# The first two weight tiles in column halves over two DMA queues, and the first output tile in one transfer

## The chip, the cores and the metric

The kernel runs on one core of one Trainium2 chip. The core has a matrix engine (TensorE, PE in the profile), whose weight loads have a row of their own (PEld), a vector engine (VectorE, DVE), a scalar engine (ScalarE, ACT), GpSimd (POOL) and a sync engine (SyncE, SP) that here only starts transfers. DMA transfers are started by SP's and by ScalarE's instruction stream; each stream works in order, so a transfer that has to wait before it may start holds back everything behind it on that stream, on ScalarE its activations too. The metric is the device time of one execution in microseconds (us).

## The reference

The reference is a decoder trunk of two layers on 256 tokens of width 1024, all in float32. Layer 0 is a feed-forward block, a gated linear recurrence, and a second feed-forward block; layer 1 is a feed-forward block, attention with a forget gate, and a second feed-forward block. Each sub-layer is normed before and after. Cut to what the change touches, the first block of layer 0 and the last sum:

```python
def rms_norm(x, g):
    y = x * lax.rsqrt(jnp.mean(x * x, axis=-1, keepdims=True) + EPS)
    return y * g

def swiglu(x, w_gate, w_up, w_down):
    return (jax.nn.silu(x @ w_gate) * (x @ w_up)) @ w_down

f = swiglu(rms_norm(h, ffn1_pre_g[layer]), ffn1_w_gate[layer], ffn1_w_up[layer], ffn1_w_down[layer])
h = h + 0.5 * rms_norm(f, ffn1_post_g[layer])
...
f = swiglu(rms_norm(h, ffn2_pre_g[layer]), ffn2_w_gate[layer], ffn2_w_up[layer], ffn2_w_down[layer])
h = h + 0.5 * rms_norm(f, ffn2_post_g[layer])
return h
```

`w_gate` and `w_up` are 1024 x 2816, `w_down` is 2816 x 1024.

## The kernel before

The 256 tokens are two row tiles, t = 0 and t = 1, of 128 tokens each. A float32 product is made of three products of rounded parts: each weight tile is loaded as `raw` and split into `whi` (a rounded copy, on ScalarE, or on VectorE where `dve=True`) and `wlo` (what the copy lost, on VectorE), and the inputs likewise into `xhi` and `xlo`; TensorE then adds whi x xhi, wlo x xhi and whi x xlo into one bank. A weight unit `i` is a `raw` tile of 128 x 1024, which for the gate weights holds two row blocks of 128 x 512 (index `a` = 0 and 1). Five `raw` buffers take turns.

Nearly all of the kernel is planned by a small cost model (`prepare_next`, `slot`, `run`), which decides when a unit is loaded and split. TensorE's order is the program's. The opening, lines 1097 to 1214, is written out by hand, in this manner:

- `load_h(t, a, b)` (line 108) loads columns of row blocks a to b of the input rows of tile t into `h[t]`; `load_w(i, a, b)` (line 1101) loads row blocks a to b of weight unit i. Lines 1106 to 1116 start them, on SP unless ScalarE's queue is named.
- `turn` (1132) transposes blocks of `h` on TensorE, `x_up` (1138) and `x_lo` (1143) make `xhi` and `xlo` of them with the gains `gT`; `w_up` (1119) and `w_lo` (1126) split the weights.
- `products(t, i, order)` (1149) issues the matmuls. In "0ul" the digit is the row block of the unit, the first letter says `whi` (u) or `wlo` (l), and the second `xhi` (u) or `xlo` (l).
- `keep_busy(n)` (121) issues n matmuls of 128 x 512 on constants, whose result nothing reads. There are six at the start and three after the first two transposes.

TensorE's stream there is: six idle matmuls, the gains' transpose, two transposes of `h[0]`, three idle matmuls, five products of (t 0, unit 0), the transposes `turn(1, 0, 2)` and `turn(1, 2, 4)` of the rows of tile 1, the sixth product, `turn(0, 2, 4)`, the six products of (1, 0), and the products of (0, 1), the first two of which read row block 0 of unit 1 and the third row block 1. ScalarE's stream is: start the load of the gains, a first activation that loads its table, start row block 1 of unit 0, start blocks 0 to 4 of `h[1]`, start row block 1 of unit 1, then the first `x_up`.

[...] In the built program the first transfers stand so (SP's and ScalarE's own order from top to bottom):

| queue | transfer | counter | must wait for |
|---|---|---|---|
| ScalarE | gains | 0 | - |
| ScalarE | unit 0, block 1 | 5 | - |
| ScalarE | h[1], blocks 0 to 4 | 7 | - |
| ScalarE | unit 1, block 1 | 1 | h[0], blocks 0 to 2 |
| SP | h[0], blocks 0 to 2 | 1 | - |
| SP | unit 0, block 0 | 2 | - |
| SP | h[0], blocks 2 to 4 | 3 | - |
| SP | unit 1, block 0 | 4 | - |
| SP | h[0], blocks 4 to 8 | 6 | - |
| SP | unit 2 | 0 | gains |
| SP | h[1], blocks 4 to 8 | 2 | unit 0, block 0 |
| SP | unit 3 | 3 | h[0], blocks 2 to 4 |

At the end `enter(t, ..., last=True)` (line 257) takes the sums of squares of the last block's output (ScalarE), the norm's factor (VectorE and GpSimd), and adds the normed product to `h[t]` in pieces (line 281), each of which is stored when it is done (line 283). Tile 0 comes some microseconds ahead of tile 1.

Of the kernel before, what the change touches and what calls it, by code (L numbers as in the profile page):

```python
# [16 lines left out]
P = 128  # L17
# [27 lines left out]
def trunk_kernel(ctx: ExitStack, tc: tile.TileContext, A: dict, out: bass.AP):  # L45
    nc = tc.nc
# [11 lines left out]
    def nm(s):  # L58
        uid[0] += 1
        return f"{s}_{uid[0]}"  # L60
# [4 lines left out]
    def gtbank():  # L65
        return psum.tile([P, 512], F32, tag="gt", name=nm("gt"), bufs=2)

    def trbank():
        return psum.tile([P, 512], F32, tag="tr", name=nm("tr"), bufs=2)
# [11 lines left out]
    def defer(n, fn):  # L81
        pend.append([n, fn])
# [23 lines left out]
    h = [hpool.tile([P, D], F32, tag=f"h{t}", name=f"h{t}") for t in range(2)]  # L106

    def load_h(t, a, b, q=nc.sync):

        q.dma_start(h[t][:, a * P:b * P], A["x"][0, t * P:(t + 1) * P, a * P:b * P])  # L110
# [10 lines left out]
    def keep_busy(n):  # L121

        ps = trbank()
        for _ in range(n):
            nc.tensor.matmul(ps, nc.const_aps.tensor(1.0, (P, P), BF16), nc.const_aps.tensor(1.0, (P, 512), BF16),
                             start=True, stop=True)
# [24 lines left out]
    def new_raw():  # L151
        return wpool.tile([P, 1024], F32, tag="raw", name=nm("raw"), bufs=RAW)
# [40 lines left out]
    def rstd_of(ss, n, f=1.0, add=nc.gpsimd):  # L193

        v = spool.tile([P, 1], F32, tag="nv", name=nm("nv"))
        add.tensor_scalar(v, ss[:, 0:1], ss[:, 1:2] if n == 2 else 0.0, D * EPS * f * f, ALU.add, ALU.add)  # L196
        r = spool.tile([P, 1], F32, tag="rstd", name=nm("rstd"), bufs=8)
        nc.gpsimd.tensor_tensor(r, v, mhalf, ALU.pow)
        return r

    def square_sum(src, acc, f=1.0):
        junk = spool.tile([P, D], BF16, tag="junk", name=nm("junk"), bufs=1)
        nc.scalar.activation(junk[:, :src.shape[1]], src, AF.Square, scale=f, accum_out=acc)  # L203

    def new_ss():
        return spool.tile([P, 2], F32, tag="ss", name=nm("ss"))

    def to_tp(src, n):

        tp = gtbank()  # L210
        for j in range(4):
            nc.tensor.transpose(tp[:, j * P:(j + 1) * P], src[:, n * 512 + j * P:n * 512 + (j + 1) * P], ident)  # L212
        return tp
# [14 lines left out]
    def to_x(tps, dest):  # L228

        with tc.high_priority():  # L230
            xg = [x_upper(tps[n], dest, n) for n in range(2)]
            for n in range(2):
                x_lower(xg[n], dest, n)

    def to_x_tiles(tps, dest):

        gi, xh, xl = dest

        def operands(k):
            return tps[k // 4][:, k % 4 * P:(k % 4 + 1) * P], gT[:, gi + k:gi + k + 1]  # L240
        with tc.high_priority():
            for k in range(8):
                src, g = operands(k)
                nc.scalar.activation(xh[:, k, :], src, AF.Copy, scale=g)
            for k in range(8):
                src, g = operands(k)
                nc.vector.scalar_tensor_tensor(xl[:, k, :], src, g, xh[:, k, :].bitcast(F32), ALU.mult, ALU.subtract)  # L247
# [4 lines left out]
    def stat(t):  # L252
        ss = new_ss()
        square_sum(h[t], ss[:, 0:1])
        rs[t] = rstd_of(ss, 1)

    def enter(t, dests, pf, gb, half, last=False, normed=False):

        f = 1.0 / 16 if half else 1.0 / 32
        ss = new_ss()  # L260
        t1 = []
        urgent = tc.high_priority()
        urgent.__enter__()
        for n in range(2):
            square_sum(pf[n], ss[:, n:n + 1], f)
        for n in range(2):
            if n == 1 and last:
                r = rstd_of(ss, 2, f, nc.vector)
            t1.append(hpool.tile([P, 512], F32, tag="t1", name=nm("t1"), bufs=2))
            nc.vector.tensor_tensor(t1[n], pf[n], gb[:, n * 512:(n + 1) * 512], ALU.mult)  # L270
        if not last:
            r = rstd_of(ss, 2, f)

        sp, aq = nc.sync, nc.scalar
        pieces = [(n * 512, 512, None) for n in range(2)]
        if last:
            pieces = ([(0, 256, sp), (256, 256, sp), (512, 512, sp)] if t == 0 else
                      [(0, 256, sp), (256, 256, aq), (512, 256, sp), (768, 256, aq)])
        for c, m, q in pieces:
            hn, tn = h[t][:, c:c + m], t1[c // 512][:, c % 512:c % 512 + m]  # L280
            nc.vector.scalar_tensor_tensor(hn, tn, r[:, 0:1], hn, ALU.mult, ALU.add)
            if last:
                q.dma_start(out[0, t * P:(t + 1) * P, c:c + m], hn)
        urgent.__exit__(None, None, None)
        if last:
            return

        def inputs():
            tps = [to_tp(h[t], n) for n in range(2)]
            for dest in dests:  # L290
                to_x(tps, dest)
            stat(t)

        def norm():
            with tc.high_priority():
                normed_x()

        def normed_x():
            ss = new_ss()
            for n in range(2):  # L300
                square_sum(h[t][:, n * 512:(n + 1) * 512], ss[:, n:n + 1])
            rs[t] = rstd_of(ss, 2)
            hn = []
            for n in range(2):
                hn.append(hpool.tile([P, 512], F32, tag="t1", name=nm("hn"), bufs=2))
                nc.vector.tensor_scalar(hn[n], h[t][:, n * 512:(n + 1) * 512], rs[t][:, 0:1], None, ALU.mult)

            def go():
                tps = []
                for n in range(2):  # L310
                    tp = gtbank()
                    for j in range(4):
                        nc.tensor.transpose(tp[:, j * P:(j + 1) * P], hn[n][:, j * P:(j + 1) * P], ident)
                    tps.append(tp)
                to_x_tiles(tps, dests[0])
            defer(6, go)

        if normed:
            norm()
            settled[0] = True  # L320
        else:
            defer(3, inputs)
# [156 lines left out]
    def ffn_items(pool_of, wg, wu, wd, post_g, next_dests, last=False, normed=False):  # L479
# [52 lines left out]
        def post_down(t, accs):  # L532
            enter(t, next_dests(t), accs, box["gb"], True, last, normed)
# [47 lines left out]
    sp = rw.tile([RT, NRT], F32, name="sp")  # L581
# [279 lines left out]
    def get_yy(t, k):  # L861
# [3 lines left out]

    row_items(A["rg_w_out"][0], [width(i) for i in range(NRT)], get_yy,
              lambda t, accs: enter(t, [main_dest(GI[("ffn2", 0)], t)], accs, gbox["mix0"], False))
    ahead(n_rg, load_gb("mix0", A["mix_post_g"][0]))
    n_wout = len(items)
# [206 lines left out]
    for n in range(2):  # L1076
        proj_items(A["attn_w_q"][0], n * 512, 512, main_x, post_q(n))
    n_q[0] = len(items)
    row_items(A["attn_w_o"][0], [P] * 8, lambda t, k: (att["oh"][t][:, k, :], att["ol"][t][:, k, :]),
              lambda t, accs: enter(t, [main_dest(GI[("ffn2", 1)], t)], accs, gbox["mix1"], False), rows0=1, late=True)  # L1080
    ahead(n_q[0] + 2, load_gb("mix1", A["mix_post_g"][1]))
    n_att = len(items)
# [16 lines left out]
    raws = [new_raw() for _ in range(OPEN)]  # L1099

    def load_w(i, a, b, q=nc.sync):

        q.dma_start(raws[i][:, a * 512:b * 512].rearrange("p (k n) -> p k n", k=b - a),
                          A["ffn1_w_gate"][0, (2 * i + a) * P:(2 * i + b) * P, :512].rearrange("(k p) n -> p k n", p=P))

    load_h(0, 0, 2)
    load_w(0, 0, 1)
    load_w(0, 1, 2, nc.scalar)
    load_h(0, 2, 4)
    load_h(1, 0, 4, nc.scalar)  # L1110
    load_w(1, 0, 1)
    load_w(1, 1, 2, nc.scalar)
    load_h(0, 4, 8)
# [18 lines left out]
    def turn(t, a, b, bank):  # L1132

        for k in range(a, b):
            tps[t, k] = bank[:, (k - a) * P:(k - a + 1) * P]
            nc.tensor.transpose(tps[t, k], h[t][:, k * P:(k + 1) * P], ident)

    def x_up(t, a, b):
        for k in range(a, b):
            nc.scalar.activation(xhi[:, k, t * P:(t + 1) * P], tps[t, k], AF.Copy,  # L1140
                                 scale=gT[:, k:k + 1])
# [19 lines left out]
    gains_T(grow0, 16, 0)  # L1161
    turn(0, 0, 1, gtbank())
    turn(0, 1, 2, gtbank())
    keep_busy(3)
    x_up(0, 0, 2)
    w_up(0, 0, 1, dve=True)
    x_lo(0, 0, 1)
# [138 lines left out]
```

## Time and profile before

| | us |
|---|---|
| median of 3 runs | 998.65 (997.85 to 998.85) |
| the profiled execution's own time | 998.38 |
| its span | 996.7 |
| TensorE busy in the span | 987.9 (99%) |
| VectorE busy | 619.2 (62%) |
| ScalarE busy | 535.8 (54%) |
| GpSimd busy | 47.6 (5%) |

The span is what the profile records, and 1.7 us of the execution lie outside it. Matmuls are pipelined: a row's duration holds the time in which a matmul drains beside the next one, so that the spacing of the starts tells how fast TensorE works. A row of the timeline gives the start, the duration, the engine (a name with a q is that engine's instruction stream, which starts transfers), the line, the operation, its tiles, how many were merged, and in brackets how long the engine had been idle and what ended that. The rows of DMA queues give packets, megabytes and the share of 16 DMA engines' time in the stretch asked for; q1 is SP's queue and q10 ScalarE's (the bytes of each match the transfers that it starts).

### The profile page before, as it was taken

The numbers are of one execution on the slowest core, as the hardware profiler recorded it, in microseconds if no ns is written. First come the engines' busy times: TensorE is split into PE (matmuls) and PEld (weight loads), VectorE is DVE, ScalarE is ACT, GpSimd is POOL, SyncE is SP. The second block draws the span as 40 slices with busy tenths as digits, with TensorE's granted clock in tenths as the row PEclk, the third lists the DMA queues.
The fourth block names the chain that finished last, engine by engine and source line by source line (L and its number), as shares of the span: only waits on it lengthen the run. The fifth ranks groups of instructions, "written<-read, shape, count | busy, mean of one in ns | idle before, by whom it ended". The sixth has DMA issues, their size and how long they took to land.

```text
span 996.7 us, 12904 instructions
## 1 busy us (share of the span) xinstructions
PE 987.9 (99%) x4776; PEld 821.1 (82%) x4776; DVE 619.2 (62%) x792; ACT 535.8 (54%) x753; POOL 47.6 (5%) x92
## 2 busy tenths in 40 slices
PE   9999999999999999999999999999999999999997
PEld 6888888899988888888898888888888788888886
DVE  6756554668997555554686655554488875555542
ACT  7546443569986544443564444444366755444431
POOL 2400000100004000000100000000020010000000
PEclk9999999999999999999999999999999999999999
DMA  8867555565336766555457666555552366665531
GB/s 285 312 187 209 187 190 189 153 194 160 109 112 218 216 183 191 189 187 188 128 202 230 184 181 186 187 188 190 170 171 64 113 205 211 190 190 190 182 115 42
DMA packets 92645, 178.89 MB, mean 179 GB/s; under 512 B 11966, under 2 KB 32614, under 8 KB 92582
## 3 DMA queue, kind: packets, MB, share of 16 engines
q1 hardware_dynamic: 90998, 176.89, 56.3%
q10 hardware_dynamic: 752, 1.06, 0.3%
q8 instruction: 37, 0.61, 0.3%
q0 software_dynamic: 832, 0.12, 0.1%
q14 instruction: 26, 0.21, 0.1%
HBM read 176.95 MB, written 1.05 MB: 179 GB/s over the span
## 4 chain that ended last, share of the span: by engine, by line
PE 95%; DMA 1%; issue 1%; DVE 1%; POOL 0%; ACT 0%; POOLq 0%; DVEq 0%; ACTq 0%
PE mm L181 28%; PE mm L183 28%; PE mm L182 28%; PE tr L508 2%; PE gt L736 2%; PE gt L1027 1%; PE mm L188 1%; PE mm L190 1%; PE mm L189 1%; PE mm L1155 1%; PE mm L1062 1%; PE tr L1048 1%; DMA raw<-in_ffn_w_gate_dram 1%; PE gt L212 1%; DMA qT<-mone 0%
## 5 line engine op out<-in xcount | busy, mean ns | idle before, releaser
L175 DVE TENSOR_TENSOR wlo<-raw,whi 128x1024 fp32r<-128x1024 f32 (+4 forms) x329 | 395.3, 1207 | 270.0 <-ACT whi L171 267.3
L171 ACT ACTIVATE whi<-raw 128x1024 fp32r<-128x1024 f32 (+4 forms) x329 | 342.0, 1045 | 312.9 <-PE mm L183 250.9
L181 PE MATMUL mm<-whi,xhi 128*128 128x512 f32 (+2 forms) x768 | 304.0, 396 | 0.0
L183 PE MATMUL mm<-whi,xlo 128*128 128x512 f32 (+2 forms) x768 | 298.8, 389 | 0.0
L182 PE MATMUL mm<-wlo,xhi 128*128 128x512 f32 (+2 forms) x768 | 298.1, 388 | 0.0
L183 PEld LDWEIGHTS mm<-whi,xlo 128*128 128x128 f32 x768 | 144.2, 188 | 30.5 <-DVE xlo L247 0.3
L182 PEld LDWEIGHTS mm<-wlo,xhi 128*128 128x128 f32 x768 | 144.4, 188 | 28.0 <-DVE wlo L175 0.3
L181 PEld LDWEIGHTS mm<-whi,xhi 128*128 128x128 f32 x768 | 144.3, 188 | 27.5
L181 PE MATMUL mm<-whi,hhi 128*128 128x512 f32 x352 | 139.1, 395 | 0.0
L183 PE MATMUL mm<-whi,hlo 128*128 128x512 f32 x352 | 137.8, 391 | 0.0
L182 PE MATMUL mm<-wlo,hhi 128*128 128x512 f32 x352 | 136.9, 389 | 0.0
L183 PEld LDWEIGHTS mm<-whi,hlo 128*128 128x128 f32 x352 | 66.1, 188 | 14.9
L182 PEld LDWEIGHTS mm<-wlo,hhi 128*128 128x128 f32 x352 | 66.1, 188 | 14.1
L181 PEld LDWEIGHTS mm<-whi,hhi 128*128 128x128 f32 x352 | 66.2, 188 | 13.1
L502 DVE SCALAR_TENSOR_TENSOR prod<-mm,rstd,sil 128x512 f32<-128x512 f32 (+1 forms) x48 | 33.9, 705 | 38.0 <-PE mm L183 34.3
L493 ACT ACTIVATE sil<-mm,rstd 128x512 f32<-128x512 f32 (+1 forms) x48 | 31.2, 652 | 40.9 <-PE mm L183 40.5
L196 POOL TENSOR_SCALAR nv<-ss 128x1 f32<-128x1 f32 x22 | 10.7, 488 | 725.7 <-ACT junk L203 725.7
L512 ACT ACTIVATE hhi<-tr 128x512 fp32r<-128x512 f32 (+1 forms) x48 | 26.6, 554 | 15.6 <-PE tr L508 15.4
L270 DVE TENSOR_TENSOR t<-mm,gb 128x512 f32<-128x512 f32 x24 | 16.2, 685 | 24.9 <-ACT junk L203 24.7
L513 DVE TENSOR_TENSOR hlo<-tr,hhi 128x512 fp32r<-128x512 f32 (+1 forms) x48 | 30.5, 641 | 1.4
L203 ACT ACTIVATE junk<-mm 128x512 bf16<-128x512 f32 x24 | 14.3, 596 | 31.5 <-PE mm L183 31.4
L181 PE MATMUL mm<-whi,zhi 128*128 128x340 f32 (+2 forms) x80 | 28.3, 354 | 0.0
(193 smaller groups left out, 910.9 us busy)
## 6 DMA issues: line engine op xcount, KB each, us to landing
raw<-in_ffn_w_down_dram SPq DMA_DIRECT2D x88, 512.0 KB
raw<-in_ffn_w_up_dram SPq DMA_DIRECT2D x80, 512.0 KB
raw<-in_ffn_w_gate_dram SPq DMA_DIRECT2D x78, 512.0 KB
raw<-in_rg_w_in_dram SPq DMA_DIRECT2D x20, 504.0 KB
raw<-in_rg_w_out_dram SPq DMA_DIRECT2D x10, 504.0 KB
raw<-in_ffn_w_gate_dram SPq DMA_DIRECT2D x18, 256.0 KB
raw<-in_ffn_w_up_dram SPq DMA_DIRECT2D x16, 256.0 KB
raw<-in_w_kv_dram SPq DMA_DIRECT2D x8, 512.0 KB
```

The costliest lines, as they stand in the source:

```text
L171: up = nc.scalar.activation(hi[:parts, c:c + m], rawv[:, c:c + m], AF.Copy)
L175: nc.vector.tensor_tensor(lo[:parts, c:c + m], rawv[:, c:c + m], hi[:parts, c:c + m].bitcast(F32), ALU.subtract)
L181: nc.tensor.matmul(ps, xh, wh, start=first, stop=False)
L182: nc.tensor.matmul(ps, xh, wl, start=False, stop=False)
L183: nc.tensor.matmul(ps, xl, wh, start=False, stop=last)
L270: nc.vector.tensor_tensor(t1[n], pf[n], gb[:, n * 512:(n + 1) * 512], ALU.mult)
L493: nc.scalar.activation(s[:, :nn], ps, AF.Silu, scale=rs[t][:, 0:1])
L502: nc.vector.scalar_tensor_tensor(pr[:, :nn], ps, rs[t][:, 0:1], s, ALU.mult, ALU.mult)
L508: nc.tensor.transpose(tp[:, j * P:(j + 1) * P], pr[:, j * P:(j + 1) * P], ident)
L512: nc.scalar.activation(hv, tp[:, :nn], AF.Copy)
L513: nc.vector.tensor_tensor(lv, tp[:, :nn], hv.bitcast(F32), ALU.subtract)
L736: nc.tensor.matmul(ps[:w, j * S:(j + 1) * S], wv[:, o:o + w], xc[:w, k, :], start=k == 0, stop=k == m - 1)
```

## The change

Three places are edited.

- Row blocks 0 and 1 of weight unit 0 (128 x 512 each) are loaded in two column halves of 256, the first half by SP and the second by ScalarE's queue. Before, SP loaded block 0 and ScalarE block 1. In the list of loads the line for `h[1]` comes ahead of that for blocks 2 to 4 of `h[0]`; they are on different queues. What is split and multiplied is as before: the first `w_up` now needs the two halves of block 0, one from each queue.
- The second `keep_busy` issues two matmuls instead of three.
- The last `enter` of tile 0 adds in two pieces of 512 columns instead of three (256, 256, 512), and stores the whole tile with one transfer of 512 KB after both, instead of one transfer per piece. Tile 1 keeps its four pieces of 256 on two queues.

On all engines the rest of the instructions stand in the order of before. [...]

| queue | transfer | counter | must wait for |
|---|---|---|---|
| ScalarE | gains | 0 | - |
| ScalarE | unit 0, block 0, second half | 5 | - |
| ScalarE | unit 0, block 1, second half | 7 | - |
| ScalarE | h[1], blocks 0 to 4 | 1 | h[0], blocks 0 to 2 |
| ScalarE | unit 1, block 1 | 3 | unit 0, block 1, first half (SP) |
| SP | h[0], blocks 0 to 2 | 1 | - |
| SP | unit 0, block 0, first half | 2 | - |
| SP | unit 0, block 1, first half | 3 | - |
| SP | h[0], blocks 2 to 4 | 4 | - |
| SP | unit 1, block 0 | 6 | - |
| SP | h[0], blocks 4 to 8 | 0 | gains |
| SP | unit 2 | 2 | unit 0, block 0, first half (SP) |
| SP | h[1], blocks 4 to 8 | 4 | h[0], blocks 2 to 4 |
| SP | unit 3 | 5 | unit 0, block 0, second half |

```diff
         pieces = [(n * 512, 512, None) for n in range(2)]
         if last:
-            pieces = ([(0, 256, sp), (256, 256, sp), (512, 512, sp)] if t == 0 else
-                      [(0, 256, sp), (256, 256, aq), (512, 256, sp), (768, 256, aq)])
+            pieces = [(0, 256, sp), (256, 256, aq), (512, 256, sp), (768, 256, aq)] if t == 1 else pieces
         for c, m, q in pieces:
             hn, tn = h[t][:, c:c + m], t1[c // 512][:, c % 512:c % 512 + m]
             nc.vector.scalar_tensor_tensor(hn, tn, r[:, 0:1], hn, ALU.mult, ALU.add)
-            if last:
+            if q:
                 q.dma_start(out[0, t * P:(t + 1) * P, c:c + m], hn)
+        if last and t == 0:
+            sp.dma_start(out[0, :P, :], h[0])
...
+    def load_w_halves(i, a):
+
+        r = slice((2 * i + a) * P, (2 * i + a + 1) * P)
+        for s, q in ((0, nc.sync), (256, nc.scalar)):
+            q.dma_start(raws[i][:, a * 512 + s:a * 512 + s + 256], A["ffn1_w_gate"][0, r, s:s + 256])
+
     load_h(0, 0, 2)
-    load_w(0, 0, 1)
-    load_w(0, 1, 2, nc.scalar)
+    load_w_halves(0, 0)
+    load_w_halves(0, 1)
+    load_h(1, 0, 4, nc.scalar)
     load_h(0, 2, 4)
-    load_h(1, 0, 4, nc.scalar)
     load_w(1, 0, 1)
     load_w(1, 1, 2, nc.scalar)
     load_h(0, 4, 8)
...
     turn(0, 0, 1, gtbank())
     turn(0, 1, 2, gtbank())
-    keep_busy(3)
+    keep_busy(2)
     x_up(0, 0, 2)
     w_up(0, 0, 1, dve=True)
```

## The prediction

> **What bounds the kernel now.** I read the page first (span, busy times, the chain that ended last), then the chain in order of time, then the first 20 us of the timeline, engine by engine, with the DMA queues' bytes by time, and last the final 12 us.
>
> ```profile
> span 996.7 us, 12904 instructions
> PE 987.9 (99%) x4776; PEld 821.1 (82%) x4776; DVE 619.2 (62%) x792; ACT 535.8 (54%) x753; POOL 47.6 (5%) x92
> PE 95%; DMA 1%; issue 1%; DVE 1%; POOL 0%; ACT 0%; POOLq 0%; DVEq 0%; ACTq 0%
> 0.80 2.60 DMA h<-in_x_dram
> 3.42 6.46 DMA raw<-in_ffn_w_gate_dram
> 9.90 0.64 ACT whi L1124
> 10.58 0.96 PE mm L1155 x3
> 5.00:6.00 1.00, 0.63 (x3) 1.00 1.03 364
> 6.00:7.00 1.00, 0.92 (x5) 1.00 0.96 283
> 10.00:11.00 1.00, 0.52 (x3) 1.00 1.05 406
> 10.50:17.50 7.00, 6.92 (x34) 1.00 0.95 351
> ```
>
> TensorE bounds it: 95% of the chain, and the chain leaves it only at the ends and in short stretches between. The opening is the one place that the change can move. There the chain goes through two transfers: `h[0]`, landed at 3.40, and what that released, ScalarE's start at 3.42 of block 1 of weight unit 1, landed 9.88. ScalarE rounds that block, and from 10.58 TensorE runs on. The four last rows (stretch, its length, TensorE's busy time, clock, DMA share, GB/s) show what a better opening could win: from 5 to 11 us TensorE is idle for 0.37, 0.08 and 0.48 us, no more. After 10.58 no wait worth a microsecond stands between the opening and the body, so a delay at 10.58 comes out at the end in full. Since the body's instructions keep their order, I cost it at no change.
>
> **Part 1: the halves and the order of starts.**
>
> ```profile
> 1.23 0.42 SPq L1103 DMA_DIRECT2D raw<-in_ffn_w_gate_dram  x1
> 1.30 0.38 ACTq L1103 DMA_DIRECT2D raw<-in_ffn_w_gate_dram  x1
> 1.70 0.42 SPq L110 DMA_DIRECT2D h<-in_x_dram  x1
> 1.71 0.45 ACTq L110 DMA_DIRECT2D h<-in_x_dram  x1
> 3.42 0.34 ACTq L1103 DMA_DIRECT2D raw<-in_ffn_w_gate_dram  x1
> 4.21 0.62 ACT L1140 ACTIVATE xhi<-gt,gT 128x128 fp32r<-128x128 f32 x2 [1.47 <-PE gt L1136]
> 4.99 0.43 DVE L1122 CAST whi<-raw 128x512 fp32r<-128x512 f32 x1 [1.01 <-DMA raw<-in_ffn_w_gate_dram]
> 5.56 0.47 PE L1155 MATMUL mm<-whi,xhi 128*128 128x512 f32 x1 [0.37 <-DVE whi L1122]
> 5.67 0.63 ACT L1124 ACTIVATE whi<-raw 128x512 fp32r<-128x512 f32 x1 [0.83 <-DMA raw<-in_ffn_w_gate_dram]
> 7.16 0.38 PE L1136 MATMUL mm<-ident,h 128*128 128x128 f32 x2
> 9.70 0.40 PE L1155 MATMUL mm<-wlo,xhi 128*128 128x512 f32 x1
> 10.58 0.50 PE L1155 MATMUL mm<-whi,xhi 128*128 128x512 f32 x1 [0.48 <-ACT whi L1124]
> q1 hardware_dynamic: 114, 0.12, 17.4%
> q1 hardware_dynamic: 562, 0.77, 44.5%
> q10 hardware_dynamic: 320, 0.53, 22.5%
> q1 hardware_dynamic: 723, 1.07, 50.8%
> q10 hardware_dynamic: 324, 0.54, 19.8%
> q10 hardware_dynamic: 464, 0.79, 22.8%
> q1 hardware_dynamic: 1106, 1.80, 57.0%
> q1 hardware_dynamic: 1317, 2.20, 61.4%
> ```
>
> (The queue rows are sums from the start of the span, in order: SP's to 2.5 us, SP's and ScalarE's to 6.5, both to 7.5, ScalarE's to 9.5, SP's to 10 and to 11.)
>
> Starts. SP issues one transfer more ahead of block 2 of `h[0]`; a step between SP's starts is 0.47 us (1.23 to 1.70), so its later unwaited starts move by that. ScalarE also starts one more; but what counts there are the new waits. `h[1]` waited for nothing and started at 1.71; now it waits for `h[0]`, which landed at 3.40, so it starts at about 3.42. Block 1 of unit 1 then waits for the first half of block 1 of unit 0 on SP, and behind it on ScalarE's stream stand the first `xhi` (4.21), through them VectorE's `xlo` and TensorE's first products.
>
> When does that half land? SP's first 0.39 MB were `h[0]` and block 0, landed at 4.98 (VectorE's 4.99); in the new order they are `h[0]` and two halves. All of unit 0 had landed at 5.65 (ScalarE's 5.67). Ends: 4.98 and 5.65. Both halves of both blocks now move together with their partners, so I take the nearer to the later, 5.4. Then ScalarE's start takes 0.34 and `xhi` begins at 5.75 in place of 4.21, and its first half (0.31) ends at 6.06. Before, the first product came 0.14 after VectorE's `whi` ended (5.42); with the same step it comes at 6.20 in place of 5.56: +0.64, from +0.2 (4.98) to +0.9 (5.65). If the half is no obstacle, the first product follows the first `whi`, which can land ahead of 4.98; block 0 was 0.26 MB, so at the 364 GB/s of the row above half of it takes 0.36 us, and the bound on the gain is -0.4.
>
> `h[1]`. Its transposes ran at 7.16 with no wait. Now it starts 1.7 us later. ScalarE's queue moved next to nothing from 6.5 to 7.5 us (320 to 324 packets), although its next transfer had been started at 3.42: the transfers run about in the order of their starts over both queues. Ahead of `h[1]` now stand the first blocks of `h[0]`, unit 0, block 2 of `h[0]` and block 0 of unit 1; with its own bytes that is 1.31 MB, and 1.57 MB with blocks 4 to 8 of `h[0]`, which start just before it. SP and ScalarE together had moved 1.30 MB at 6.5 and 1.61 at 7.5. A transfer lands somewhat later than its bytes move: ScalarE's 0.79 MB were moved by 9.5 and landed at 9.88, 0.4 later. So `h[1]` lands between 6.9 and 7.9, with the slower packets of the next paragraph (0.3) at 8.2 at the latest, and TensorE comes to it at 7.16 + 0.64 = 7.80. The wait is 0 to 0.4; I take 0.2, its middle. Together the sixth product and all behind move by 0.84. From 7.16 to the end of the products before the wait at 10.58 is 2.77 us of TensorE's work (to 9.93, with 0.23 us a product), so TensorE arrives at 10.77.
>
> The transfer that sets 10.58. The bytes ahead of block 1 of unit 1 are the same. But 256 packets of 2 KB become 512 of 1 KB. From the queue rows, a 1 KB packet took 0.174 x 16 x 2.5 / 114 = 61 ns of an engine, and a 2 KB packet (0.614 x 16 x 11 - 0.570 x 16 x 10) / 211 = 80 ns. The difference is (512 x 61 - 256 x 80) / 16 = 0.67 us on each engine. The engines were not all full so early, so the ends are 0 and 0.67 and I take the middle, 0.3: it lands at 10.2, and its product comes at 10.9. That is later than 10.77, so it sets the end: +0.3.
>
> The last loads of the opening (units 2 and 3, `h[1]`'s second half) are late by the same 0.3; their cover is that TensorE is full from 11 to 17 us. Where it is gone, at the wait in the stretch 10.5 to 17.5 (0.08 idle), I add 0.1, with ends 0 and 0.3. Sum of part 1: +0.4, from -0.9 (gain at 5.56 and the 0.48 at 10.58 gone) to +1.2.
>
> [...]
>
> **Part 2: one idle matmul less.**
>
> ```profile
> 1.21 0.15 PEld L125 LDWEIGHTS <-const-bfloat16-1.0 128*128 128x128 bf16 x1 [0.27 <-issue]
> 1.64 0.15 PEld L125 LDWEIGHTS <-const-bfloat16-1.0 128*128 128x128 bf16 x1 [0.28 <-issue]
> 4.17 1.02 PE L125 MATMUL tr<-const-bfloat16-1.0 128*128 128x512 bf16 x3
> 8.33 0.40 PE L1155 MATMUL mm<-wlo,xhi 128*128 128x512 f32 x1
> 8.56 0.39 PE L1155 MATMUL mm<-whi,xhi 128*128 128x512 f32 x1
> ```
>
> The three ended at 5.19, ahead of the 5.56, so the removed one saves nothing. But a matmul of 512 columns takes 0.43 us at 1.21 and 0.23 at 8.33: TensorE starts at half speed and becomes fast somewhere around the three. Without the third it stands from about 4.9 to 6.2 where it stood from 5.19 to 5.56. If it was fast by then, that costs 0, which I take, since all three fit into 1.02 us, less than 3 x 0.43. The other end is the first rival.
>
> **Part 3: the output.**
>
> ```profile
> L281 DVE SCALAR_TENSOR_TENSOR h<-t,rstd,h x27: 479/745/753, 185.4 to 993.4; 128x512 f32<-128x512 f32 x21, 128x256 f32<-128x256 f32 x6
> 985.38 1.54 DVE L281 SCALAR_TENSOR_TENSOR h<-t,rstd,h 128x256 f32<-128x256 f32 x3
> 988.62 0.69 DVE L270 TENSOR_TENSOR t<-mm,gb 128x512 f32<-128x512 f32 x1 [1.70 <-ACT junk L203]
> 992.76 1.12 SPq L283 DMA_DIRECT2D out_dram<-h  x2
> ```
>
> Tile 0's sum takes 2 x 0.745 = 1.49 us in place of 1.54, ahead of VectorE's next work at 988.62. Its transfer starts near 986.9, with the 512 KB still some 6 us ahead of SP's next start at 992.76, and at 364 GB/s they take 1.4 us. Cost 0; the cover would have to lose 4 us before it cost anything.
>
> **The sum.** The profiled execution took 998.38 (1.68 outside its span), 0.27 below the median of the runs. 998.38 + 0.4 = 998.8 against its own time, and against the median 998.65 + 0.4 = 999.05. I predict **999.0**; its own range is 997.75 to 999.85 (-0.9 to +1.2). A change under 0.2% (2.0 us) is about what a measurement of this kernel cannot tell from none.
>
> **The rivals.**
>
> *The slow clock lasts longer (slower).* If TensorE's change to full speed needs the stretch that the third matmul filled, the products from 6.2 us go at 0.43 each. The 2.77 us of work up to 10.58 become 2.77 x 0.43 / 0.23 = 5.2, which is 2.4 more; with the first five products, about 1.1 us at full speed, another 1.0. Of these 3.4 us, the gap from TensorE's arrival (10.77) to the forecast's 10.9 hides 0.1; so 999.05 + 3.3 = 1002.3 at most, and where the change of speed comes halfway, 1000.7. It decides against me when over half of those products are slow. For it: 1.3 us idle in place of 0.37. Against it: the three that fit into 1.02. Chance 0.2. [...]
>
> *The halves pay (faster, but hardly).* Block 0 lands 0.4 us earlier, and the first half's wait is short. Then the first product comes at 5.2, and the gaps of 0.37, 0.08 and 0.48 close: 998.65 - 0.9 = 997.75. For it: VectorE waited for the transfer until 4.99. Against it: `xhi` behind a waiting start. Chance 0.14, and more than 2.0 us are not to be had in the opening, as the idle time adds up to 0.93.
>
> *All hidden.* The delays end in the 0.48 us before 10.58, and the transfer that sets it lands as before: 998.65. Chance 0.14.
>
> A body that runs differently, for a reason that I do not see, gets 0.09 on both sides together; the forecast keeps 0.43.
>
> **How the numbers follow.** The range 997.7 to 1001.2 leaves out the longer half of the slow clock (0.1) and a body that moves far (0.09). Slower by over 0.2% (above 1000.65) is 0.17 of the slow clock and 0.04 of such a body: 0.21. Faster by over 0.2% (below 996.65) is the other 0.05 of it. Within: 0.43 + 0.14 + 0.14 and the 0.03 of the slow clock that stays below, 0.74.
>
> **What would show it.** In the changed kernel: ScalarE's start of `h[1]` just after `h[0]` lands, its next start between 5.0 and 5.7 and the first `xhi` behind it; the first product later than 5.56; products on unit 0 with starts 0.23 apart (0.43 would be the slow clock); the product that followed at 10.58 now near 10.9; the last 12 us the same, shifted. The prediction is wrong if TensorE is idle over 2 us in the opening, or if the body's stretches differ.

## The result and the profile after

| | before | changed |
|---|---|---|
| median of 8 runs each, us | 998.55 (997.50 to 998.85) | 1000.92 (999.03 to 1003.12) |
| profiled execution, us | 998.38 | 1000.87 |
| its span, us | 996.7 | 999.2 |
| ratio, 95% interval | | 1.0027 (1.0017 to 1.0036) |

The changed kernel is slower. I had forecast no difference that can be measured, so the forecast was wrong; 999.0 was named, and the ends of that case's own range were 997.75 and 999.85. Only the wider range of 997.7 to 1001.2, with the rivals in it, holds 1000.92.

First the row that says where to look. The view by operation gives for each group the count, the shortest, median and longest duration in ns, and the first and last start. The three L181 to L183 lines carry the body. Of the kernel before:

```profile
L181 PE MATMUL mm<-whi,xhi x768: 314/389/579, 19.5 to 933.2; 128*128 128x512 f32 x180, 128*128 128x504 f32 x8, 128*128 128x336 f32 x4
```

Of the changed kernel, with the page's totals:

```profile
span 999.2 us, 12902 instructions
PE 989.4 (99%) x4775; PEld 822.4 (82%) x4775; DVE 619.4 (62%) x791; ACT 535.8 (54%) x753; POOL 47.6 (5%) x92
L181 PE MATMUL mm<-whi,xhi x768: 314/389/579, 22.2 to 935.7; 128*128 128x512 f32 x180, 128*128 128x504 f32 x8, 128*128 128x336 f32 x4
```

From the first of these matmuls to the last it is 913.7 us before and 913.5 after. The whole difference of 2.5 us arises ahead of 22.2 us. The start of the first L181 matmul therefore serves below as the length of the opening: 19.5 before, 22.2 here. It is read from one execution of each kernel.

The chain of the changed kernel in order of time (start, length, what) now goes through the transfer of `h[1]`; before, its second transfer was block 1 of weight unit 1:

```profile
0.80 2.52 DMA h<-in_x_dram
3.33 5.66 DMA h<-in_x_dram
9.04 0.69 PE mm L1143 x2
```

The changed kernel's timeline (start, duration, engine, operation; in brackets the idle time and what ended it):

```profile
4.12 0.43 DVE L1129 CAST whi<-raw 128x512 fp32r<-128x512 f32 x1
...
5.50 0.33 ACTq L1104 DMA_DIRECT2D raw<-in_ffn_w_gate_dram  x1
5.94 0.63 ACT L1147 ACTIVATE xhi<-gt,gT 128x128 fp32r<-128x128 f32 x2 [3.19 <-DMA raw<-in_ffn_w_gate_dram]
...
6.36 0.51 PE L1162 MATMUL mm<-whi,xhi 128*128 128x512 f32 x1 [1.12 <-ACT xhi L1147]
...
7.71 0.39 PE L1162 MATMUL mm<-whi,xlo 128*128 128x512 f32 x1
...
9.04 0.69 PE L1143 MATMUL mm<-ident,h 128*128 128x128 f32 x2 [0.94 <-DMA h<-in_x_dram]
...
11.23 0.63 PE L1162 MATMUL mm<-wlo,xhi 128*128 128x512 f32 x1
...
11.66 0.63 PE L1162 MATMUL mm<-whi,xhi 128*128 128x512 f32 x1
...
12.94 0.39 PE L1162 MATMUL mm<-whi,xhi 128*128 128x512 f32 x1
...
13.39 0.40 PE L1162 MATMUL mm<-whi,xhi 128*128 128x512 f32 x1
```

There are three losses in it, read one after another. First, VectorE rounds block 0 at 4.12 in place of 4.99, so that block did land earlier, but nobody could use it: `xhi` stands behind ScalarE's start at 5.50, which waited for SP's half, and the first product comes at 6.36 in place of 5.56 (+0.80). Second, the transposes of `h[1]` wait for their transfer until 9.04 in place of 7.16 (+1.88, of which 1.08 are new). As `h[1]` landed at 8.99 (3.33 + 5.66), they would have come at 9.04 with an early first product too: the +0.80 is part of the +1.88 and does not add to it, which is why the chain does not pass through it. Third, the matmuls at 11.23 and 11.66 are 0.43 apart, where such matmuls were 0.23 apart before (8.33 and 8.56): TensorE has fallen to about half speed. What took 2.31 us before (7.16 to 9.47) takes 3.90 (9.04 to 12.94): +1.59. The product that stood at 10.58 comes at 13.39 (+2.81, less than 1.88 + 1.59 because the wait ahead of it is gone), and a small part of that is made up by 22.2.

The view by stretches shows the fall (stretch, its length, TensorE's busy time, granted clock, DMA share, GB/s), again of the changed kernel:

```profile
5.60:9.00 3.40, 1.74 (x5) 1.00 1.00 346
9.00:12.40 3.40, 3.36 (x11) 0.50 1.03 381
```

In 3.4 us TensorE was busy for half the time; in the next 3.4 us its clock was 0.50 (0.96 in the 0.2 us ahead of 9.0, 1.00 from 12.4 on), after which the starts are 0.23 apart again. The slow stretch was 3.4 us long in this execution, and the clock fell when TensorE had been idle for 1.66 of the 3.4 us ahead of it. What decides that it falls, this execution alone doesn't show.

The end of the changed kernel: tile 0's sum in two pieces, its one transfer, tile 1's pieces and their transfers.

```profile
987.88 1.42 DVE L280 SCALAR_TENSOR_TENSOR h<-t,rstd,h 128x512 f32<-128x512 f32 x2
989.32 0.35 SPq L284 DMA_DIRECT2D out_dram<-h  x1
...
995.26 1.12 SPq L282 DMA_DIRECT2D out_dram<-h  x2
```

It begins 2.50 later than before (985.38), and SP's last starts come 2.50 later too (992.76): the same end, shifted.

### The profile page after: what moved, and what is told of

Its sections match the earlier page's. It is cut to its first block, busy times and chain, and to the rows that moved or that the text cites. A ratio compares the mean times of both kernels' runs of the same rounds, so it can differ in the third digit from the quotient of the medians.

```text
span 999.2 us, 12902 instructions
## 1 busy us (share of the span) xinstructions
PE 989.4 (99%) x4775; PEld 822.4 (82%) x4775; DVE 619.4 (62%) x791; ACT 535.8 (54%) x753; POOL 47.6 (5%) x92
## 4 chain that ended last, share of the span: by engine, by line
PE 98%; DMA 1%; issue 1%; ACT 0%; DVE 0%; POOLq 0%; POOL 0%; DVEq 0%; ACTq 0%
PE mm L181 29%; PE mm L183 28%; PE mm L182 28%; PE tr L509 2%; PE gt L737 2%; PE mm L1162 1%; PE gt L1028 1%; PE mm L188 1%; PE mm L190 1%; PE mm L189 1%; DMA h<-in_x_dram 1%; PE mm L1063 1%; PE gt L212 1%; PE tr L1049 1%; PE tr L924 0%
## 5 line engine op out<-in xcount | busy, mean ns | idle before, releaser
L181 PE MATMUL mm<-whi,xhi 128*128 128x512 f32 (+2 forms) x768 | 304.0, 396 | 0.0
L183 PE MATMUL mm<-whi,xlo 128*128 128x512 f32 (+2 forms) x768 | 298.8, 389 | 0.0
L183 PEld LDWEIGHTS mm<-whi,xlo 128*128 128x128 f32 x768 | 144.2, 188 | 30.4 <-DVE xlo L247 0.3
L181 PEld LDWEIGHTS mm<-whi,xhi 128*128 128x128 f32 x768 | 144.3, 188 | 27.5
L181 PE MATMUL mm<-whi,hhi 128*128 128x512 f32 x352 | 139.1, 395 | 0.0
L183 PE MATMUL mm<-whi,hlo 128*128 128x512 f32 x352 | 137.8, 391 | 0.0
L183 PEld LDWEIGHTS mm<-whi,hlo 128*128 128x128 f32 x352 | 66.1, 188 | 14.9
L181 PEld LDWEIGHTS mm<-whi,hhi 128*128 128x128 f32 x352 | 66.2, 188 | 13.1
L181 PE MATMUL mm<-whi,zhi 128*128 128x340 f32 (+2 forms) x80 | 28.3, 354 | 0.0
```

The source lines that it names most:

```text
L181: nc.tensor.matmul(ps, xh, wh, start=first, stop=False)
L183: nc.tensor.matmul(ps, xl, wh, start=False, stop=last)
```

## The experiments

The theory to be tested: with two transfers more ahead of them, `h[1]` and block 1 of unit 1 get new waits and start late (3.33 in place of 1.71, 5.50 in place of 3.42), and the gaps that this opens in TensorE's work cost time twice, as waits and, in some executions, as half speed. The rivals: the idle matmul that was removed; the new output; the halves themselves, with their smaller packets. In each experiment nothing of the computation is left out or altered; where transfers or matmuls are added, nothing reads what they give. The ratio is to the kernel before, run beside it, with its 95% interval.

### The idle matmul alone, and the output alone

The kernel before with one edit:

```diff
-    keep_busy(3)
+    keep_busy(2)
```

> The kernel before with the second group of idle matmuls cut from three to two and nothing else. Theory W (the changed kernel lost its time by new waits of two starts on ScalarE's queue, which leave TensorE idle at 5.2 to 6.4 and 8.1 to 9.0 us and so halve its clock from 9.0 to 12.4): the waits are not here, the gap before the first product grows from 0.37 to about 0.8 us only, so 998.55, within 0.4 of the kernel before, and no stretch at half clock after the first product. Theory K (the missing idle matmul itself costs the clock): stretches at clock 0.50 between 5 and 13 us as in the changed kernel, 999.7 to 1000.9.

Measured: 998.56 (11 runs), ratio 0.9998 (0.9990 to 1.0007). The opening is 19.7 long and no stretch of it after 5 us is slow.

The kernel before with the change's lines in `enter` and nothing else:

```diff
+            pieces = [(0, 256, sp), (256, 256, aq), (512, 256, sp), (768, 256, aq)] if t == 1 else pieces
...
+        if last and t == 0:
+            sp.dma_start(out[0, :P, :], h[0])
```

> The kernel before with tile 0's output summed in two pieces and stored in one transfer, and nothing else. All theories about the opening: 998.55, within 0.3, the last start of tile 0's output near 987 us and the last 4 us unchanged. If the output had a part in the 2.4 us: 999 or more, with a later end after the last sum.

Measured: 998.37 (11 runs), ratio 1.0002 (0.9993 to 1.0010). Neither of the two edits makes a measurable difference by itself.

### The loads alone, and the waits alone

The loads alone: the changed kernel with three idle matmuls and the old output.

```diff
-    keep_busy(2)
+    keep_busy(3)
```

> The changed kernel with the three idle matmuls and the old output pieces put back, so that only the loads differ from before. Theory W: 1000.9 as the changed kernel, within 0.8, with the wide spread of its runs and a stretch at half clock near 9 to 12 us. Theory K: the third idle matmul keeps the clock, about 999.5 (the waits without the clock).

The waits alone: the kernel before, with whole blocks, three idle matmuls and the old output, and two transfers of 2 KB, one on each queue, at the place of the second halves; they are to bring the late starts without the halves.

```diff
     load_w(0, 1, 2, nc.scalar)
+    tiny = cpool.tile([P, 8], F32, name="tiny")
+    nc.sync.dma_start(tiny[:, :4], A["x"][0, :P, :4])
+    nc.scalar.dma_start(tiny[:, 4:], A["x"][0, :P, 4:8])
```

> The kernel before with whole blocks as it had them, and two tiny transfers of 2 KB (nothing reads them), one on each queue, at the place where the second halves stand in the changed kernel. [...] Theory W: ScalarE's first rounding of the inputs starts after 5 us, h[1] lands after 8 us, TensorE idles there, the clock falls, 1000.5 (999.7 to 1001.5). Theory H (the halves themselves, their smaller packets and their landing in pairs, cost it): 998.7, within 0.4.

Measured: the loads 1000.07 (11 runs), ratio 1.0019 (1.0010 to 1.0028); the waits 1000.54 (10 runs), ratio 1.0021 (1.0012 to 1.0030). The timeline of the second (the last row is ScalarE's rounding of block 1 of unit 1):

```profile
5.48 0.33 ACTq L1103 DMA_DIRECT2D raw<-in_ffn_w_gate_dram  x1
5.92 0.63 ACT L1143 ACTIVATE xhi<-gt,gT 128x128 fp32r<-128x128 f32 x2 [3.19 <-DMA tiny<-in_x_dram]
6.34 0.50 PE L1158 MATMUL mm<-whi,xhi 128*128 128x512 f32 x1 [0.99 <-ACT xhi L1143]
...
8.27 0.44 PE L1139 MATMUL mm<-ident,h 128*128 128x128 f32 x2 [0.18 <-DMA h<-in_x_dram]
...
10.94 0.63 ACT L1127 ACTIVATE whi<-raw 128x512 fp32r<-128x512 f32 x1 [0.89 <-DMA raw<-in_ffn_w_gate_dram]
```

ScalarE's start, `xhi` and the first product stand within 0.02 us of where they stand in the changed kernel (5.50, 5.94, 6.36), and `h[1]` is started at 3.42 (there 3.33), though no block is halved: two transfers that move 4 KB together bring a loss of the same size. `h[1]` came earlier in this execution (a wait of 0.18); what sets the end of its opening is block 1 of unit 1, whose product comes at 11.63 in place of 10.58. The opening is 20.3 long with the loads, 20.6 with the waits, and neither profile has a slow stretch. So in these two executions the waits by themselves lengthen the opening by 0.8 and 1.1 us. The medians are 1.65 and 2.12 above those of before (998.42); what makes up the rest, these two executions don't show.

### The changed kernel again, twice

No edit; the second is also the control of the runs with filled gaps below.

> The changed kernel unaltered, beside the next three on one chip. 1000.9 (1000.2 to 1001.5), with runs from 999 to 1003. Theory W+K (the waits cost about 1.6 and, only together with them, the missing idle matmul lets the clock fall in about half of the executions): about half of the runs have a granted clock of 0.997 or less over the span. If the clock has no part, the spread of the clocks is that of the kernel before (0.998 to 1.000).

> The changed kernel a third time: 1000.2 (999.7 to 1000.9), with some executions at 0.997 or less.

Measured: 999.89 (11 runs), ratio 1.0012 (1.0004 to 1.0021), and 1000.25 (11 runs), ratio 1.0017 (1.0008 to 1.0026). The loss is confirmed, and 1.0027 was the largest of three readings. The openings are 20.6 and 20.7 long. Timeline and stretches of the first:

```profile
8.95 0.44 PE L1143 MATMUL mm<-ident,h 128*128 128x128 f32 x2 [1.51 <-DMA h<-in_x_dram]
...
10.19 0.39 PE L1162 MATMUL mm<-wlo,xhi 128*128 128x512 f32 x1
10.42 0.40 PE L1162 MATMUL mm<-whi,xhi 128*128 128x512 f32 x1
5.20:8.90 3.70, 1.75 (x5) 1.00 0.96 325
8.90:12.40 3.50, 3.45 (x18) 1.00 1.05 403
```

TensorE was busy for 1.75 us in 3.7, as little as in the execution shown above, and did not slow down. So the waits are in all three profiles of this kernel (for `h[1]` 0.94, 1.51 and, in the third, 1.27) and the half speed after them only in the one above. Why one execution falls to it and another doesn't, no run here shows.

Over all 30 runs of the changed kernel the median is 1000.25. In 11 of them the mean granted clock was 0.997 or less; their median is 1000.87, that of the other 19 is 999.89. The kernel before, beside all experiments, had 998.59 (135 runs, 4 of them with such a clock). By this the waits cost about 1.3 us (999.89 - 998.59), and the half speed adds 0.4 to the median (1000.25 - 999.89) and most of the runs above 1001. The split is rough: a mean clock doesn't say where in the execution the clock fell, and it leaves out the half speed with which these executions start (products 0.43 apart until 12.1 at a mean clock of 0.998 in the kernel without idle matmuls, below). Other runs put the waits elsewhere: the kernel with the waits alone lost 2.1 with one run of 10 at such a clock, and the kernels with filled gaps, next, lose 0.9.

### The gaps filled

The changed kernel with idle matmuls in both gaps, so that TensorE is busy while it waits:

```diff
-    keep_busy(2)
+    keep_busy(7)
...
     products(0, 0, "0uu 0ul 1uu 0lu 1ul")
+    keep_busy(3)
```

> The changed kernel with seven idle matmuls in place of two ahead of the first product and three more after the fifth product, so that TensorE works in both of its gaps (5.2 to 6.4 and 8.1 to 9.0); the waits stay. Theory W+K: no execution falls to clock 0.50 after 6 us, all clocks 0.998 to 1.000, 999.9 (999.5 to 1000.4) with the spread of the kernel before. Theory W alone (the clock is a bystander): 1000.9 as the changed kernel.

> The changed kernel with both gaps filled by idle matmuls, a second time, beside the changed kernel. If the clock has a share: 0.3 to 1.0 below the changed kernel, and no execution with a granted clock of 0.997 or less. If not: the same as the changed kernel.

Measured: 999.59, ratio 1.0005 (0.9996 to 1.0014), and 999.72, ratio 1.0009 (1.0000 to 1.0018), 11 runs each. In none of the 22 was the granted clock 0.997 or less, and the longest took 1000.57, where the changed kernel reaches 1003.12. The timeline of the first shows what is left, with no slow stretch after 4.08 us (clock 1.00, products 0.23 apart at 9.36) and a wait for block 1 of unit 1 at the end; in the second it is the wait for `h[1]` again (0.54):

```profile
4.08 1.69 PE L125 MATMUL tr<-const-bfloat16-1.0 128*128 128x512 bf16 x7
...
7.29 0.82 PE L125 MATMUL tr<-const-bfloat16-1.0 128*128 128x512 bf16 x3
8.12 0.44 PE L1143 MATMUL mm<-ident,h 128*128 128x128 f32 x2
...
11.46 0.63 ACT L1131 ACTIVATE whi<-raw 128x512 fp32r<-128x512 f32 x1 [1.57 <-DMA raw<-in_ffn_w_gate_dram]
```

With useless work in the gaps the falls of the clock and the long runs are gone; the waits stay, as they must (the openings are 21.1 and 20.6 long). This shows that the gaps bring the falls. How much time the falls cost in the middle is not shown: the medians are 0.3 and 0.5 below those of the changed kernel beside them, but the intervals of the ratios overlap.

### One wait taken away at a time

`h[1]` started ahead of ScalarE's halves, so that it waits for nothing:

```diff
     load_h(0, 0, 2)
+    load_h(1, 0, 4, nc.scalar)
     load_w_halves(0, 0)
     load_w_halves(0, 1)
-    load_h(1, 0, 4, nc.scalar)
```

> The changed kernel with the start of h[1]'s first half put ahead of ScalarE's two halves, so that it waits for nothing; now ScalarE's half of block 1 waits for h[0], and unit 1's block 1 waits as in the changed kernel, with the first rounding of the inputs behind it. Theory h (the late h[1] is the larger part): no wait at the transposes of h[1] at all, 999.4 (999.0 to 1000.0). Theory x (the late rounding of the inputs is the larger part): 1000.3 or more.

Measured: 1002.35 (6 runs), ratio 1.0033 (1.0021 to 1.0045). I had missed that block 1's second half would then land late. Timeline and stretches:

```profile
8.06 0.63 ACT L1131 ACTIVATE whi<-raw 128x512 fp32r<-128x512 f32 x1 [1.20 <-DMA raw<-in_ffn_w_gate_dram]
8.74 0.80 PE L1162 MATMUL mm<-whi,xhi 128*128 128x512 f32 x1 [1.21 <-ACT whi L1131]
8.00:9.00 1.00, 0.26 (x1) 0.50 1.06 356
12.00:13.00 1.00, 1.00 (x4) 0.50 1.07 406
```

TensorE waits for that half instead, and the clock stays at half until at least 13 us. The opening is 23.9 long, and 4 of the 6 runs had a clock of 0.997 or less.

Block 1 of unit 1 started by SP, so that ScalarE's stream waits for nothing but `h[1]`:

```diff
-    load_w(1, 1, 2, nc.scalar)
+    load_w(1, 1, 2)
```

> The changed kernel with unit 1's block 1 started by SP, so that no long wait stands ahead of the first rounding of the inputs on ScalarE; the start of h[1] still waits for h[0]. Theory h: the first product comes by 5.3 us and TensorE then waits for h[1] for over 1.5 us, 1000.2 or more, the clock falling in some runs. Theory x: 999.4 (999.0 to 1000.0).

Measured: 999.12 (11 runs), ratio 1.0012 (1.0003 to 1.0021), as the changed kernel in the same comparison. `xhi` is early again (4.54), and in the profile TensorE waits the longer for `h[1]`:

```profile
7.34 0.63 PE L1162 MATMUL mm<-wlo,xhi 128*128 128x512 f32 x1
7.77 0.63 PE L1162 MATMUL mm<-whi,xlo 128*128 128x512 f32 x1
...
9.84 0.69 PE L1143 MATMUL mm<-ident,h 128*128 128x128 f32 x2 [1.44 <-DMA h<-in_x_dram]
```

That execution took 1001.39 and is not a typical one: the two products are 0.43 apart, and TensorE ran at half speed from its start until 13.3. The median of 999.12 lies where I had expected it if the late `xhi` were the larger part (999.0 to 1000.0), 0.8 below that of the changed kernel beside it; the equal ratios don't confirm that.

In both, the wait removed was replaced by another. The shares of the two waits in the loss can't be told apart this way.

The same edit made to the kernel before takes away the only wait in ScalarE's first starts there:

> The kernel before with unit 1's block 1 started by SP right behind block 0, at about 2.6 us in place of 3.4 and ahead of the second half of h[0] and of unit 2. If the transfer that ends last before 10.58 is what the opening of the kernel before waits for, it lands near 8.5, the wait of about 0.5 to 0.9 goes, 998.0 (997.6 to 998.5). Rival: the transfers behind it (h[0] blocks 4 to 8, unit 2) come later and take its place: 998.6.

> The kernel before with unit 1's block 1 on SP behind block 0, a second time, because the first time (0.9996, from 0.9987 to 1.0005) left open whether it is faster. The opening's trace was 0.75 us shorter there. If that is the gain: 997.7 (997.2 to 998.2); if not: 998.4.

Measured: 997.81, ratio 0.9996 (0.9987 to 1.0005), and 997.93, ratio 0.9994 (0.9985 to 1.0003), 11 runs each. The product of 10.58 comes at 9.94 in the first profile and the opening is 18.8 long, 0.7 less; in the second it is at 10.25 and 19.1, with a first product as late as 6.08. The medians are lower by 0.6 and 0.7, but both intervals contain 1: it isn't shown to beat the kernel before.

### The halves without the waits

The changed kernel with `h[1]` on GpSimd's queue; ScalarE's early starts then have no new wait (ScalarE starts block 1 of unit 1 at 3.53 and 3.36 in the two runs and `xhi` at 4.21 and 4.20; before, 3.42 and 4.21):

```diff
-    load_h(1, 0, 4, nc.scalar)
+    load_h(1, 0, 4, nc.gpsimd)
```

> [...] Theory W: 998.6 (998.1 to 999.1), the first rounding of the inputs at 4.2 to 4.6 us, no wait at the transposes of h[1], no clock below 0.998. Theory H (halves and their packets cost something of their own): 999.2 or more.

> The halves without the waits, a second time, beside its control. 999.1 (998.5 to 999.6); if the halves cost nothing, within 0.3 of the control.

And its control, with whole blocks: the kernel before with the two small transfers, `h[1]` on GpSimd's queue and two idle matmuls, so that the queues and the number of transfers are the same (ScalarE starts block 1 of unit 1 at 3.90 and `xhi` at 4.52).

```diff
+    nc.sync.dma_start(tiny[:, :4], A["x"][0, :P, :4])
+    nc.scalar.dma_start(tiny[:, 4:], A["x"][0, :P, 4:8])
...
-    load_h(1, 0, 4, nc.scalar)
+    load_h(1, 0, 4, nc.gpsimd)
...
-    keep_busy(3)
+    keep_busy(2)
```

> [...] If the halves cost something of their own: 998.5 here and about 0.5 more in the next run. If what is left there is h[1] on GpSimd's queue: 999.1 in both.

Measured: the halves 999.17, ratio 1.0009 (1.0000 to 1.0018), and 999.89, ratio 1.0005 (0.9996 to 1.0014); the whole blocks 998.96, ratio 1.0005 (0.9996 to 1.0014); 11 runs each. The second run of the halves:

```profile
6.49 0.63 ACT L1131 ACTIVATE whi<-raw 128x512 fp32r<-128x512 f32 x1 [1.66 <-DMA raw<-in_ffn_w_gate_dram]
7.17 0.50 PE L1162 MATMUL mm<-whi,xhi 128*128 128x512 f32 x1 [1.33 <-ACT whi L1131]
L181 PE MATMUL mm<-whi,xhi x768: 314/389/579, 19.6 to 933.6; 128*128 128x512 f32 x180, 128*128 128x504 f32 x8, 128*128 128x336 f32 x4
```

With the first product at 4.96 there, a new gap opens ahead of block 1, and yet the opening is 19.6 long, as before. The profiled execution of the whole blocks, at half speed until about 9.5 and with an opening of 20.3, can't be held against it. A cost of the halves themselves isn't shown: the ratios beside each other are equal. It isn't excluded either: the medians beside each other differ by 0.9, where I had allowed 0.3. Nor is a gain shown, with the waits out of the way. The whole blocks without the waits (1.0005) against those with them, the waits alone (1.0021), show once more what the waits cost; the two kernels differ in the queue of `h[1]` and in one idle matmul.

### No idle matmuls in the first gap

The changed kernel without the second `keep_busy`. If the removed idle matmul had a part in the clock's falls, leaving out the other two should bring more of them.

```diff
-    keep_busy(2)
```

> The changed kernel with the second group of idle matmuls left out altogether, so that TensorE is idle from about 4.2 us to its first product. Theory W+K (beside the waits the share of executions that fall to half clock counts, and idle matmuls ahead of the gap lower it): more executions at a granted clock of 0.997 or less than the 7 of 19 of the changed kernel, median 1001 or more. Theory W alone: 1000.2 as the changed kernel's 19 runs together, since the removed matmuls stand in front of no work.

Measured: 1000.43 (11 runs), ratio 1.0016 (1.0007 to 1.0025). Runs with a clock of 0.997 or less: 2 of 11 with none, 11 of 30 with two, 2 of 11 with three (the loads alone). That goes neither up nor down with the number of idle matmuls. But the mean clock leaves out half speed at the start of an execution. The profiled execution took 1000.85 with a mean clock of 0.998, and its products are 0.43 apart, where nothing stands between them, until 12.1:

```profile
8.32 0.63 PE L1162 MATMUL mm<-wlo,xhi 128*128 128x512 f32 x1
8.75 0.63 PE L1162 MATMUL mm<-whi,xlo 128*128 128x512 f32 x1
```

So the rival as I had forecast it, a late first switch to full speed, does occur in kernels with these waits (here and with unit 1 on SP), and no run shows in how many executions. A part of the removed matmul in that or in the falls isn't shown, nor excluded.

## Why the prediction was wrong

- **Where the change acts: right.** The starts came as read from the tables of waits: `h[1]` at 3.33 (forecast 3.42), ScalarE's next start at 5.50 (5.4, between 5.0 and 5.7), `xhi` at 5.94 (5.75), the first product at 6.36 (6.20). With 1.12 and 0.94 us TensorE is idle for just over the 2 us that I had named as a sign of being wrong. The body and the end didn't change, parts 2 and 3 alone cost nothing that can be measured (0.9998 and 1.0002).
- **The wait for `h[1]`: the mis-sized term.** Forecast 0.2 (0 to 0.4), with a landing between 6.9 and 8.2. It landed at 8.99 here, and TensorE waited 0.94; in the two repeats 1.51 and 1.27. The queues of the changed kernel (packets, MB, share; both to 7.5 us, then both to 8.5):

```profile
q1 hardware_dynamic: 859, 1.05, 45.3%
q10 hardware_dynamic: 437, 0.50, 22.0%
...
q1 hardware_dynamic: 1037, 1.40, 50.8%
q10 hardware_dynamic: 467, 0.54, 21.0%
```

  ScalarE's bytes up to and with `h[1]` are 0.53 MB (gains, two halves, 256 KB). By the order of the starts I had let at most 1.57 MB pass in all, at about 7.4, and taken the landing 0.4 later. The bulk kept to that: by 7.5 the two queues had moved 1.55 MB, 0.50 of them ScalarE's. But the last 0.03 MB of `h[1]` took until about 8.4, while SP's later transfers moved another 0.3, and the landing came some 0.5 after them. What failed is the step from the bytes to the landing: I took one transfer to be finished before the next begins, and here the late start shared its end with SP's transfers.
- **Block 1 of unit 1 as what sets the end: wrong here.** Forecast +0.3 at 10.58, with a landing at 10.2. As `h[1]` was that late, in the execution shown TensorE reached that product (13.39) with no wait for the block, and the delay at `h[1]` went through to the end. Where `h[1]` or the gaps cost less, the block does set the end, but later than forecast: it landed at 10.92 with the waits alone and at 11.44 in the first profile with filled gaps. The upper end of the sum, +1.2, doesn't follow from its terms either: 0.67 for the block and 0.3 for the last loads make 0.97.
- **The clock: a term put at nothing, the rival's mechanism at another place.** I asked whether the first switch to full speed would come late for want of one idle matmul, and gave it 0.2. Leaving out that matmul alone costs nothing that can be measured (0.9998). But the waits that I had myself put into the sum open two gaps within some 4 us, and I didn't ask what they do to a clock that is already full. They halve it in some executions; in the one shown (0.50 from 9.0 to 12.4) that costs 1.6 us (2.31 to 3.90), more than the whole forecast of +0.4.
- **One execution for all.** The prediction summed one execution against a kernel whose three runs lay within 1.0 us, and took that for steadiness. Its 135 later runs go from 997.16 to 1001.16, and the 30 of the changed kernel from 999.03 to 1003.12; from one profile to another both landings and clock differ. "All hidden" and "the halves pay" fell: block 0's earlier rounding (4.12) had no `xhi` to go with, and in the kernels without the new waits the halves show no gain over the whole blocks (1.0005 each, beside each other).

What stays open: how an added transfer brings the new waits (the runs show only that it does), how much the waits cost without the clock (0.9 to 2.1 us by different runs) and how that divides between them, whether the removed idle matmul takes part in the clock's falls or in a late first switch, how often that switch is late, and whether the kernel before with block 1 of unit 1 on SP is faster by the 0.6 us of its medians.

## What to carry to other kernels

Two added transfers of 2 KB each were enough here to move later starts (block 1 of unit 1 to 5.48 from 3.42): list which earlier transfer each later start must wait for, and what stands behind that start on its engine (here `xhi`, at 5.92 in place of 4.21). Where a stream is full, give a transfer that starts late a landing among all that moves then, and not only behind the starts ahead of it (`h[1]` landed at 8.99 here, where I had 8.2 at the latest). And when a sum contains new gaps of about 1 us in TensorE's work near one another, price the clock's fall too (here 1.6 us more in the execution shown, and a mean clock of 0.997 or less in 11 of 30), as work that nobody needs covered it here (none of 22 with the gaps filled). Read the speed from the spacing of the matmuls too, and not from the clock alone.

## What the runs showed of the hardware that I had not expected

The first switch to full speed came at different times in executions with the same opening. In the profile of the output alone, whose opening is that of before, the products are still 0.43 apart at 7 us, and remain so until about 9.6, while before they were at full speed from 5.6 (0.31 apart at 5.56, 0.23 at 6.69):

```profile
6.64 0.63 PE L1156 MATMUL mm<-whi,xlo 128*128 128x512 f32 x1
7.07 0.63 PE L1156 MATMUL mm<-whi,xhi 128*128 128x512 f32 x1
...
7.00:8.00 1.00, 1.00 (x4) 1.00 1.03 344
```

The clock column reads 1.00 in that stretch, so it doesn't show the half speed from which these executions start; the spacing of the matmuls does (0.43 here, 0.23 before at 8.33). In the profiles of the whole blocks without waits, the kernel without idle matmuls and the changed kernel with unit 1 on SP the first switch came at about 9.5, 12.1 and 13.3. The runs of the output alone are no slower than those of before, so such openings are presumably among the runs of before as well.

The clock also fell far behind the opening. In the kernel before with block 1 of unit 1 on SP, the profiled execution gave its gain back at 740 us; that stretch, and below it the same one in the kernel before:

```profile
740.00:745.00 5.00, 3.54 (x17) 0.84 0.02 7
```

```profile
740.00:745.00 5.00, 4.09 (x24) 1.00 0.08 24
```

TensorE idles there in both kernels (for 1.46 and 0.91 us of the 5), and only in one of the two executions did the clock follow.
